# One block for TensorE's loop, a thirteenth turn, shorter programs, and octets loaded in pairs

## The chip, the cores and the metric

The kernel runs on one core of a Trainium2 chip. The metric is device time in microseconds for one execution; the time before is a median of three runs. The profile is of one further execution, and every duration below is from it unless another source is named.

## The reference

Linear attention with a ReLU feature map, on 8 batches x 12 heads, 512 positions, 64 dimensions, in float32:

```python
Q_feat = np.maximum(0, Q)
K_feat = np.maximum(0, K)
KV = np.einsum('bhkd,bhkv->bhdv', K_feat, V)
K_sum = np.sum(K_feat, axis=2)
numerator = np.einsum('bhqd,bhdv->bhqv', Q_feat, KV)
denominator = np.einsum('bhqd,bhd->bhq', Q_feat, K_sum)
return (numerator / (denominator[:, :, :, None] + 1e-10)).astype(np.float32)
```

## The kernel before, in words

The 96 heads are worked in twelve octets of eight heads (NO = 12). One octet of Q, K or V is 1 MiB in float32, laid out as 128 partitions of 32 rows each, so a partition holds 8 KB of the source and sixteen partitions hold one head. Q, K and V come in as bf16 (cast by the DMA), except K and V of octet 0, which come in as float32 on SyncE's and ScalarE's queues into output buffers that are not yet in use. All other loads go out on GpSimd's queue, one octet at a time (RUNS = (1,) * 11): three DMAs, K, V and Q, into a ring of six slots (RING); a load waits until the octet that used its slot has been consumed (semaphores PR1, VC, STG). Stores go out on GpSimd's queue too, except the last two, which SyncE issues. HEAD sets how many stores are put between the loads: in before, store 0 stands ahead of load 10 and store 1 ahead of load 11, and all others follow the last load. NOUT is the number of output buffers; norm(o) waits for store o - NOUT.

The program is written out by hand, engine by engine, with semaphores. There is no scheduler.

VectorE works in this order for each octet o: prep(o + 1, 0) masks the first half of K and part of V (after CK0, TensorE's sign that it is through with the buffers); stage(o + 1) copies Q to q_sb (STG); norm(o - 1) multiplies the transposed result by the reciprocals, in two halves (NRM0, NRM1), after TensorE's transposes (CB0, CB1); denominators(o) makes the reciprocals; prep(o + 1, 1) does the second halves (PR1). What stands behind a wait on VectorE waits too.

TensorE runs a hardware loop of twelve turns (lines 189 and 190). A turn transposes q_sb (16 matmuls, line 158), accumulates K'V in two halves of 32 (line 167), transposes back the result of the octet before (back, 16 matmuls, line 148, after OT), computes the denominators (line 176) and the numerators in two halves (line 184, after NRM0 and NRM1). After the loop stand two more back calls for the last octet. The loop's first instruction is placed at slot 0 of a block of 256 instructions (head_slot).

ScalarE evacuates the transposes of Q with the ReLU (line 214), K'V (line 219) and the numerators (ot, line 228), and masks a part of V (line 208).

At the end SyncE alone waits for the twelve store semaphores (line 318) and clears the semaphores; the other engines run off the end of their programs when their own work is done.

Of the kernel before, what the change touches and what calls it, by code (L numbers as in the profile page):

```python
# [5 lines left out]
def kernel(  # L6
# [5 lines left out]
):  # L12
    nc = tc.nc

    tc.close()
    tc.compile()

    B, H, S, D = Q.shape
    assert D == 64
    P = 128  # L20
    D1, D4 = D + 1, D + 4
    R = S * 4 // P
    RQ = 2 * R
    U = RQ // 2
    NO = B * H // 8
    assert NO * 8 == B * H and R == 16
    RING = 6
    NOUT = 9
    RUNS = (1,) * 11
    HEAD = 4  # L30

    fp32 = mybir.dt.float32
    bf16 = mybir.dt.bfloat16
    Act = mybir.ActivationFunctionType
    Alu = mybir.AluOpType
    PE, PL, VE, AC, SP = nc.tensor, nc.gpsimd, nc.vector, nc.scalar, nc.sync
# [6 lines left out]
    def sb(name, shape, dt):  # L43
        return nc.alloc_sbuf_tensor(name, shape, dt)[:]
# [3 lines left out]
    def sems(*names):  # L48
        new = [nc.alloc_semaphore(n) for n in names]
        handles.extend(new)  # L50
        return new

    ident = sb("ident", [P, P], bf16)
    ident32 = sb("ident32", [P, P], fp32)
    mask_k = sb("mask_k", [P, 2], fp32)
    mask_v = sb("mask_v", [P, 2], fp32)
    mask_h = sb("mask_h", [P, 8, 2], fp32)
    k_all = sb("k_all", [P, RING, RQ, D], bf16)
    v_all = sb("v_all", [P, RING, RQ, D], bf16)
    q_all = sb("q_all", [P, RING + 1, U * P], bf16)  # L60
    o_sb = [sb(f"o_sb{i}", [P, RQ, D], fp32) for i in range(NOUT)]
    k8, v8 = o_sb[0], o_sb[1]
# [1 line left out]
    q_sb = sb("q_sb", [P, U, P], bf16)  # L64
    qt_sb = sb("qt_sb", [P, U, P], bf16)
    kf = [sb(f"kf{i}", [P, R, 2, D], bf16) for i in range(2)]
    vo = [sb(f"vo{i}", [P, R, 2, D4], bf16) for i in range(2)]
    kvd = sb("kvd", [P, 8, 2 * D1], bf16)
    ot = sb("ot", [P, U, 8, 16], fp32)
    own = sb("own", [P, U, 8, 2], fp32)  # L70
# [10 lines left out]
    ID, STG, PR0, PR1, DEN, NRM0, NRM1, DV = sems(  # L81
        "id", "stg", "pr0", "pr1", "den", "nrm0", "nrm1", "dv")
    VC, KVD, OT = sems("vc", "kvd", "ot")
    CQ0, CQ1, CK0, CK1, CB0, CB1, CD, CO0, CO1 = sems(
        "cq0", "cq1", "ck0", "ck1", "cb0", "cb1", "cd", "co0", "co1")
    landed = {}
    stored = sems(*[f"st{o}" for o in range(NO)])

    def land(name):
        landed[name], = sems(name)  # L90
        return landed[name]


    SP.dma_start(out=k8.rearrange("p r d -> p (r d)"), in_=Kr[0]).then_inc(land("k0"), 16)
# [4 lines left out]
    def slot(o):  # L99
        return (o - 1) % RING if o > 0 else RING  # L100
# [13 lines left out]
    def store(eng, o):  # L114
        eng.wait_ge(NRM1, o + 2)
        kw = {"single_packet": True} if eng is PL else {}
        eng.dma_start(out=Or[o], in_=o_sb[(o + 2) % NOUT].rearrange("p r d -> p (r d)"), **kw).then_inc(stored[o], 16)  # L117

# [4 lines left out]
    o, done = 1, 0  # L123
    for n in RUNS:
        while done < o + n - 1 - RING - HEAD + 1:
            store(PL, done)
# [3 lines left out]
    assert o == NO  # L130
    for i in range(done, NO - 2):
        store(PL, i)
    for i in range(NO - 2, NO):
        store(SP, i)

# [2 lines left out]
    def arrived(eng, c, o):  # L138
        s = landed[f"{c}{run_of[o]}"]
        if (eng.engine, s.num) not in seen:  # L140
            seen.add((eng.engine, s.num))
            eng.wait_ge(s, 16)

    def back(j):
        for v in range(8):
            t = PE.transpose(ps_o[j][:, P * v:P * v + P], ot[:, 8 * j + v].rearrange("p h c -> p (h c)"), ident32)  # L148
        t.then_inc((CB0, CB1)[j], 1)
# [35 lines left out]
                              start=True, stop=True, skip_group_check=True)  # L185
            t.then_inc((CO0, CO1)[j], 1)

    PE.wait_ge(ID, 4)
    with nc.Fori(1, NO + 1, engines=bass.OrderedEngineSet([PE.engine]), head_slot={PE.engine: 0}) as i:
        turn(i)  # L190
    PE.wait_ge(OT, NO + 1)
    back(0)
    back(1)


    def v_rows(o, g):
        rows = slice(R * g, R * g + R)
        return v_all[:, slot(o), rows] if o > 0 else v8[:, rows]

    def k_rows(o, g):  # L200
        rows = slice(R * g, R * g + R)
        return k_all[:, slot(o), rows] if o > 0 else k8[:, rows]

    def v_scalar(o):
        arrived(AC, "v", o)
        if o == 0:
            AC.wait_ge(ID, 4)
        AC.activation(vo[0][:, :, 1, 2:D + 2], v_rows(o, 0), Act.Copy, scale=mask_v[:, 1:2]).then_inc(VC, 1)  # L208

    v_scalar(0)  # L210
    for o in range(NO):
        for j in range(2):
# [4 lines left out]
        for s in range(2):  # L217
            for c in range(2):
                t = AC.copy(  # L219
                    kvd[64 * c:64 * c + 64, s::2, c * D1:c * D1 + D1].rearrange("p (g t) d -> p g t d", t=2),  # L220
                    ps_kv[64 * s:64 * s + 64, :, 0:2 * (D + 2)].rearrange(
                        "p g (t d) -> p g t d", t=2)[:, :, :, c:c + D1])
# [3 lines left out]
        for j in range(2):  # L226
            AC.wait_ge((CO0, CO1)[j], o + 1)
            t = AC.copy(ot[:, :, 4 * j:4 * j + 4],  # L228
                        ps_o[j].rearrange("p (h u c) -> p u h c", h=4, u=U))
        t.then_inc(OT, 1)  # L230


    def prep(o, g):

        arrived(VE, "k", o)
        for s in range(2):
            VE.tensor_scalar(kf[g][:, :, s, :], k_rows(o, g), scalar1=0.0,  # L237
                             scalar2=mask_k[:, s:s + 1], op0=Alu.max, op1=Alu.mult)
        arrived(VE, "v", o)
        for t in range(1 + g):  # L240
            x = VE.tensor_scalar(vo[g][:, :, t, 2:D + 2], v_rows(o, g), scalar1=mask_v[:, t:t + 1],  # L241
                                 scalar2=None, op0=Alu.mult)
        x.then_inc((PR0, PR1)[g], 1)

    def stage(o):
        arrived(VE, "q", o)
        VE.tensor_copy(q_sb.rearrange("p u f -> p (u f)"), q_all[:, slot(o)]).then_inc(STG, 1)  # L247

    def norm(o):
        dst = o_sb[(o + 2) % NOUT]  # L250
        if o >= NOUT:
            VE.wait_ge(stored[o - NOUT], 16)
        VE.wait_ge(DV, 2 * o + 2 + DV0)
        if o == NOUT - 1:
            VE.wait_ge(VC, 1)
        for j in range(2):
            rs = slice(R * j, R * j + R)
            VE.wait_ge((CB0, CB1)[j], o + 2)
            VE.tensor_tensor(dst[:, rs], ps_o[j].rearrange("p (r d) -> p r d", d=D),  # L259
                             rec[o % 2][:, rs].unsqueeze(2).to_broadcast([P, R, D]),  # L260
                             op=Alu.mult).then_inc((NRM0, NRM1)[j], 1)

    def denominators(o):
        VE.wait_ge(CD, o + 1)
        VE.scalar_tensor_tensor(
            own.rearrange("p u h c -> p u (h c)"), ps_den.rearrange("p u h c -> p u (h c)"), 1e-10,
            mask_h.rearrange("p h c -> p (h c)").unsqueeze(1).to_broadcast([P, U, 16]),
            op0=Alu.add, op1=Alu.mult).then_inc(DEN, 1)
        VE.wait_ge(DEN, o + 2)
        VE.tensor_reduce(out=den.rearrange("p (u c) -> p u c", c=2), in_=own.rearrange("p u h c -> p u c h"),  # L270
                         op=Alu.add, axis=mybir.AxisListType.X).then_inc(DV, 1)
        VE.wait_ge(DV, 2 * o + 1 + DV0)
        VE.reciprocal(rec[o % 2], den).then_inc(DV, 1)

    for t in range(2):
        VE.memset(mask_v[:, t:t + 1], 0.0)
    VE.memset(kvd.rearrange("p h d -> p (h d)").bitcast(fp32), 0.0)
    VE.memset(ot.rearrange("p u h c -> p (u h c)"), 0.0).then_inc(OT, 1)
    ones = [vo[g][:, :, :, 1:D4 - 1][:, :, :, 0:D + 2:D1] for g in range(2)]
    VE.memset(ones[0], 0.0)  # L280
    VE.memset(ones[1], 0.0).then_inc(DV, 1)
    VE.wait_ge(DV, 1)
    for t in range(2):
        for half in range(2):
            b = 64 * half + 32 * t
            VE.memset(mask_v[b:b + 32, t:t + 1], 1.0)
            for g in range(2):
                VE.memset(ones[g][b:b + 32, :, t], 1.0)
    VE.wait_ge(ID, 2)
    VE.tensor_copy(ident32, ident).then_inc(ID, 1)  # L290
    VE.wait_ge(ID, 3)
    for c in range(2):
        VE.tensor_reduce(out=mask_h[:, :, c], in_=ident32.rearrange("p (h b) -> p h b", h=8),
                         op=Alu.add, axis=mybir.AxisListType.X)
    VE.tensor_reduce(out=mask_k, in_=ident32.rearrange("p (t s b) -> p s t b", t=4, s=2),
                     op=Alu.add, axis=mybir.AxisListType.XY).then_inc(ID, 1)
    DV0 = 1
    VE.wait_ge(ID, 4)
    for s in (DEN, NRM0, NRM1):
        VE.sem_inc(s, 1)  # L300
    prep(0, 0)
    prep(0, 1)
    stage(0)
    for o in range(NO):
        if o + 1 < NO:
            VE.wait_ge(CK0, o + 1)
            prep(o + 1, 0)
            stage(o + 1)
        if o > 0:
            norm(o - 1)  # L310
        denominators(o)
        if o + 1 < NO:
            prep(o + 1, 1)
    norm(NO - 1)


    for s in stored:
        SP.wait_ge(s, 16)
    used = sorted(s.num for s in handles)
    assert used == list(range(used[0], used[-1] + 1))  # L320
    SP.sem_clear(range(used[0], used[-1] + 1))
# [28 lines left out]
```

## Time and profile before

| What | Value |
|---|---|
| Median of three runs | 124.86 us (124.73 to 124.92) |
| Profiled execution, its time | 124.66 us |
| Its span (first to last instruction) | 123.4 us |
| Granted TensorE clock, mean | 0.941 |
| Busy: TensorE, VectorE, ScalarE, GpSimd | 71%, 72%, 64%, 22% |
| DMA | 32.57 MB moved in packets; HBM read 37.75 MB, written 12.58 MB |
| Loads on GpSimd's queue, issue to landing | 33 to 37 us (median by tensor) |
| SyncE's wait for the last stores (line 318) | 5.8 us |

The page gives for each engine the busy time and a row of 40 slices of the span; the DMA row is the mean busy share of the core's 16 DMA engines. A cast load is counted by the bytes that it writes, so that 213 GB/s in the middle of the row stand for twice as much read from HBM. Line numbers are those of the kernel before.

### The profile page before, as it was taken

Reading aid. Unit: us, or ns where it says so; the run is one execution under the profiler, and the core shown is the slowest. Engines: PE = TensorE matmul, PEld = TensorE weight load, DVE = VectorE, ACT = ScalarE, POOL = GpSimd, SP = SyncE. Lnnn points to the kernel's source line nnn. Section 1 sums busy time; section 2 is a strip of 40 time slices with the busy share of each in tenths; the row PEclk is TensorE's granted clock in tenths of the full one; section 3 lists DMA queues with packets and bytes.
Section 4 is the critical chain, followed back from the end, with each engine's and each line's share of the span. In section 5 each row is a group of like instructions: output and inputs, shape, how many; then the busy total and the mean of one; then the engine's idle time right before and its main releaser. Section 6 shows DMA issues by size and latency. Waiting matters only on the chain.

```text
span 123.4 us, 3380 instructions
## 1 busy us (share of the span) xinstructions
PE 87.4 (71%) x1456; PEld 75.9 (62%) x1456; DVE 89.3 (72%) x178; ACT 79.4 (64%) x109; POOL 27.5 (22%) x50
## 2 busy tenths in 40 slices
PE   0000099998998979799897998979449939977400
PEld 0000099986886868688686877958429928947200
DVE  3737906599989899998989989897395497091600
ACT  0043063999988888898888889888539649542000
POOL 3999500050240804309101001010010001000000
PEclk9999999999999999999999999999985995996775
DMA  3999999999999999999999999999999999999994
GB/s 43 369 344 217 213 213 213 213 215 213 214 213 213 213 215 213 214 214 217 214 213 214 213 214 221 371 217 214 375 222 214 343 425 428 425 422 433 420 425 170
DMA packets 6918, 32.57 MB, mean 264 GB/s; under 512 B 768, under 2 KB 768, under 8 KB 5120
## 3 DMA queue, kind: packets, MB, share of 16 engines
q0 software_dynamic: 6336, 28.31, 92.2%
q1 hardware_dynamic: 432, 3.15, 6.6%
q10 hardware_dynamic: 144, 1.05, 2.2%
q8 instruction: 2, 0.03, 0.1%
q14 instruction: 4, 0.03, 0.1%
HBM read 37.75 MB, written 12.58 MB: 408 GB/s over the span
## 4 chain that ended last, share of the span: by engine, by line
DMA 34%; issue 27%; POOL 18%; PE 8%; DVE 5%; ACT 1%; POOLq 0%; DVEq 0%
DMA q_all<-in_Q_dram 34%; POOL k_all L109 6%; POOL q_all L109 5%; POOL v_all L109 5%; DVE o_sb L259 5%; PE ps_o L148 4%; PE ps_kv L167 2%; PE ps_q L158 1%; PE ps_o L184 1%; POOL out_dram L117 1%; ACT ot L228 1%; POOL q_all L96 1%; POOL ident L121 0%; POOL ident L119 0%; POOLq L107 0%
## 5 line engine op out<-in xcount | busy, mean ns | idle before, releaser
L259 DVE TENSOR_TENSOR o_sb<-ps_o,rec 128x1024 f32<-128x1024 f32 x24 | 28.3, 1219 | 7.0 <-PE ps_o L148 6.7
L228 ACT COPY ot<-ps_o 128x1024 f32<-128x1024 f32 x24 | 24.2, 1013 | 10.3 <-PE ps_o L184 9.2
L167 PE MATMUL ps_kv<-vo,kf 64*128 64x132 bf16 x768 | 28.6, 230 | 0.7
L148 PE MATMUL ps_o<-ident,ot 128*128 128x128 f32 x208 | 27.1, 286 | 1.1 <-ACT ot L228 1.1
L167 PEld LDWEIGHTS ps_kv<-vo,kf 64*128 64x128 bf16 x768 | 24.8, 100 | 3.8 <-DVE vo L241 2.3
L214 ACT ACTIVATE qt_sb<-ps_q 128x1024 bf16<-128x1024 bf16 x24 | 23.4, 1030 | 5.1 <-PE ps_q L158 5.1
L158 PE MATMUL ps_q<-ident,q_sb 128*128 128x128 bf16 x192 | 15.3, 243 | 15.4 <-DVE q_sb L247 15.4
L148 PEld LDWEIGHTS ps_o<-ident,ot 128*128 128x128 f32 x208 | 23.8, 146 | 2.7 <-ACT ot L228 1.4
L158 PEld LDWEIGHTS ps_q<-ident,q_sb 128*128 128x128 bf16 x192 | 13.2, 110 | 16.7 <-DVE q_sb L247 15.4
L219 ACT CAST kvd<-ps_kv 64x260 bf16<-64x260 f32 x48 | 18.0, 375 | 7.8 <-PE ps_kv L167 7.4
L184 PE MATMUL ps_o<-qt_sb,kvd 128*128 128x256 bf16 x96 | 15.0, 282 | 10.8 <-DVE o_sb L259 9.8
L237 DVE TENSOR_SCALAR kf<-k_all,mask_k 128x1024 bf16<-128x1024 bf16 x44 | 18.3, 459 | 5.6 <-PE ps_kv L167 5.4
L184 PEld LDWEIGHTS ps_o<-qt_sb,kvd 128*128 128x128 bf16 x96 | 7.7, 100 | 15.6 <-DVE o_sb L259 15.0
L241 DVE TENSOR_SCALAR vo<-v_all,mask_v 128x1024 bf16<-128x1024 bf16 x33 | 15.0, 483 | 0.9 <-DMA v_all<-in_V_dram 0.9
L109 POOL DMA_DIRECT2D k_all<-in_K_dram x11 | 8.4, 763 | 32.1 <-DVE vo L241 32.0
L117 POOL DMA_DIRECT2D out_dram<-o_sb x10 | 5.3, 533 | 40.7 <-DVE o_sb L259 40.7
L208 ACT ACTIVATE vo<-v_all,mask_v 128x1024 bf16<-128x1024 bf16 x11 | 12.7, 1155 | 0.3
L247 DVE COPY q_sb<-q_all 128x2048 bf16<-128x2048 bf16 x12 | 8.3, 694 | 5.7 <-DMA q_all<-in_Q_dram 5.7
L109 POOL DMA_DIRECT2D q_all<-in_Q_dram x11 | 8.9, 811 | 0.0
L109 POOL DMA_DIRECT2D v_all<-in_V_dram x11 | 7.6, 687 | 0.0
L176 PE MATMUL ps_q<-kvd,qt_sb 128*128 128x16 bf16 x192 | 6.9, 180 | 0.0
L176 PEld LDWEIGHTS ps_q<-kvd,qt_sb 128*128 128x128 bf16 x192 | 6.7, 96 | 0.2
(24 smaller groups left out, 27.8 us busy)
## 6 DMA issues: line engine op xcount, KB each, us to landing
out_dram<-o_sb POOLq DMA_DIRECT2D x10, 1024.0 KB, 39.8
q_all<-in_Q_dram POOLq DMA_DIRECT2D x12, 512.0 KB, 36.7
k_all<-in_K_dram POOLq DMA_DIRECT2D x11, 512.0 KB, 33.1
v_all<-in_V_dram POOLq DMA_DIRECT2D x11, 512.0 KB, 34.8
out_dram<-o_sb SPq DMA_DIRECT2D x2, 1024.0 KB, 8.4
o_sb<-in_K_dram SPq DMA_DIRECT2D x1, 1024.0 KB, 8.5
o_sb<-in_V_dram ACTq DMA_DIRECT2D x1, 1024.0 KB, 8.8
```

Of the source, the lines that this page charges most:

```text
L109: PL.dma_start(out=t[:, to:to + n], in_=X[o:o + n].rearrange("n p f -> p n f"), single_packet=True).then_inc(land(f"{c}{o}"), 16)
L148: t = PE.transpose(ps_o[j][:, P * v:P * v + P], ot[:, 8 * j + v].rearrange("p h c -> p (h c)"), ident32)
L158: t = PE.transpose(dst[:, u], q_sb[:, j * (U // 2) + u], ident)
L167: t = PE.matmul(ps_kv[:, half, 0:2 * (D + 2)].rearrange("p (t d) -> p t d", t=2), kf[g][rows, r].rearrange("p s d -> p (s d)"), vo[g][rows ...
L176: t = PE.matmul(ps_den[:, u], qt_sb[:, u], kvd[:, :, 0:2 * D1:2 * D1 - 1], start=True, stop=True, skip_group_check=True)
L184: t = PE.matmul(ps[:, h], kvd[:, 4 * j + h, 1:2 * D + 1], q[:, :, 4 * j + h, :], start=True, stop=True, skip_group_check=True)
L214: AC.activation(qt_sb[:, j * (U // 2):(j + 1) * (U // 2)], ps_q[j].bitcast(bf16).rearrange("p (u f) -> p u f", u=U // 2), Act.Relu)
L219: t = AC.copy(kvd[64 * c:64 * c + 64, s::2, c * D1:c * D1 + D1].rearrange("p (g t) d -> p g t d", t=2), ps_kv[64 * s:64 * s + 64, :, 0:2 * ...
L228: t = AC.copy(ot[:, :, 4 * j:4 * j + 4], ps_o[j].rearrange("p (h u c) -> p u h c", h=4, u=U))
L237: VE.tensor_scalar(kf[g][:, :, s, :], k_rows(o, g), scalar1=0.0, scalar2=mask_k[:, s:s + 1], op0=Alu.max, op1=Alu.mult)
L241: x = VE.tensor_scalar(vo[g][:, :, t, 2:D + 2], v_rows(o, g), scalar1=mask_v[:, t:t + 1], scalar2=None, op0=Alu.mult)
L259: VE.tensor_tensor(dst[:, rs], ps_o[j].rearrange("p (r d) -> p r d", d=D), rec[o % 2][:, rs].unsqueeze(2).to_broadcast([P, R, D]), op=Alu. ...
```

## The change

The program of each engine is altered, not what is computed.

- TensorE: an alignment to a block of 256 instructions is put ahead of the opening barrier, so that barrier, loop and end stand in one block; the alignment at the loop head and the wait on ID ahead of it go. The loop has thirteen turns, and the last octet's back calls are those of turn 13. So that turn 13 can pass its waits, VectorE raises STG, PR0 and PR1 once more after the last denominators, and ScalarE raises KVD and VC after its last copy.
- VectorE: the masks of V and the ones beside V are made with one reduction and one copy instead of sixteen memsets; three semaphore increments ride on instructions that are there anyway; norm waits for DV only for the last octet, and prep waits for DV at its second V mask instead. The program goes from 211 to 186 instructions.
- GpSimd: octets 3 and 4, 5 and 6, 7 and 8 are loaded two by two, one DMA each for K, V and Q of a pair (RUNS); one store (HEAD 5) instead of two stands ahead of the last loads. The program goes from 68 to 59 instructions.
- NOUT goes from 9 to 11. Stores 1 to 9 share the semaphore ALL, stores 10 and 11 share LAST.
- End: TensorE, ScalarE, VectorE and GpSimd wait for all stores too (hold) and raise FIN; SyncE waits for FIN.

```diff
+    nc.tensor.addr_align(256, offset=0, max_nops=0)
     tc.close()
     tc.compile()
...
-    NOUT = 9
-    RUNS = (1,) * 11
-    HEAD = 4
+    NOUT = 11
+    RUNS = (1, 1, 2, 2, 2, 1, 1, 1)
+    HEAD = 5
...
-    vo = [sb(f"vo{i}", [P, R, 2, D4], bf16) for i in range(2)]
+    vo_all = sb("vo", [P, 2, R, 2, D4], bf16)
+    vo = [vo_all[:, i] for i in range(2)]
...
-    stored = sems(*[f"st{o}" for o in range(NO)])
+    ALL, LAST, FIN = sems("all", "last", "fin")
+    stored = [sems(f"st{o}")[0] if o + NOUT < NO else ALL if o < NO - 2 else LAST for o in range(NO)]
...
+    def hold(eng):
+        eng.wait_ge(ALL, 16 * (NOUT - 2))
+        eng.wait_ge(LAST, 32)
+        eng.sem_inc(FIN, 1)
...
+    hold(PL)
...
-    PE.wait_ge(ID, 4)
-    with nc.Fori(1, NO + 1, engines=bass.OrderedEngineSet([PE.engine]), head_slot={PE.engine: 0}) as i:
+    with PE.Fori(1, NO + 2) as i:
         turn(i)
-    PE.wait_ge(OT, NO + 1)
-    back(0)
-    back(1)
+    hold(PE)
...
+    AC.wait_ge(KVD, NO)
+    AC.wait_ge(VC, NO)
+    AC.sem_inc(KVD, 1)
+    AC.sem_inc(VC, 1)
+    hold(AC)
...
         for t in range(1 + g):
+            if t and o:
+                VE.wait_ge(DV, 2 * o + DV0)
...
-        VE.wait_ge(DV, 2 * o + 2 + DV0)
+        if o == NO - 1:
+            VE.wait_ge(DV, 2 * o + 2 + DV0)
...
-    for t in range(2):
-        VE.memset(mask_v[:, t:t + 1], 0.0)
...
+    VE.tensor_reduce(out=mask_v, in_=ident32.rearrange("p (a t b) -> p t a b", a=2, t=2),
+                     op=Alu.add, axis=mybir.AxisListType.XY).then_inc(ID, 1)
...
+    VE.tensor_copy(vo_all.rearrange("p g r t d -> p (g r) t d")[:, :, :, 1:D4 - 1][:, :, :, 0:D + 2:D1],
+                   mask_v.unsqueeze(1).unsqueeze(3).to_broadcast([P, 2 * R, 2, 2])).then_inc(ID, 1)
...
+    for s in (STG, PR0, PR1):
+        VE.wait_ge(s, NO)
+        VE.sem_inc(s, 1)
     norm(NO - 1)
-    for s in stored:
-        SP.wait_ge(s, 16)
+    hold(VE)
+    SP.wait_ge(CO1, NO + 1)
+    SP.wait_ge(FIN, 4)
```

More of the change, by code (lines that the diff above doesn't have):

```diff
@@ L206, in v_scalar @@
         if o == 0:
-            AC.wait_ge(ID, 4)
+            AC.wait_ge(ID, 5)
         AC.activation(vo[0][:, :, 1, 2:D + 2], v_rows(o, 0), Act.Copy, scale=mask_v[:, 1:2]).then_inc(VC, 1)
@@ L273, in denominators @@
         VE.reciprocal(rec[o % 2], den).then_inc(DV, 1)
-    for t in range(2):
-        VE.memset(mask_v[:, t:t + 1], 0.0)
-    VE.memset(kvd.rearrange("p h d -> p (h d)").bitcast(fp32), 0.0)
+    VE.memset(kvd.rearrange("p h d -> p (h d)").bitcast(fp32), 0.0).then_inc(DEN, 1)
     VE.memset(ot.rearrange("p u h c -> p (u h c)"), 0.0).then_inc(OT, 1)
[L279 to L288, printed above, removed]
     VE.wait_ge(ID, 2)
@@ L291 @@
     VE.wait_ge(ID, 3)
-    for c in range(2):
-        VE.tensor_reduce(out=mask_h[:, :, c], in_=ident32.rearrange("p (h b) -> p h b", h=8),
-                         op=Alu.add, axis=mybir.AxisListType.X)
+    VE.tensor_reduce(out=mask_v, in_=ident32.rearrange("p (a t b) -> p t a b", a=2, t=2),
+                     op=Alu.add, axis=mybir.AxisListType.XY).then_inc(ID, 1)
     VE.tensor_reduce(out=mask_k, in_=ident32.rearrange("p (t s b) -> p s t b", t=4, s=2),
-                     op=Alu.add, axis=mybir.AxisListType.XY).then_inc(ID, 1)
-    DV0 = 1
+                     op=Alu.add, axis=mybir.AxisListType.XY).then_inc(NRM0, 1)
+    VE.tensor_reduce(out=mask_h, in_=ident32.rearrange("p (h b) -> p h b", h=8).unsqueeze(2).to_broadcast([P, 8, 2, 16]),
+                     op=Alu.add, axis=mybir.AxisListType.X).then_inc(NRM1, 1)
     VE.wait_ge(ID, 4)
-    for s in (DEN, NRM0, NRM1):
-        VE.sem_inc(s, 1)
+    VE.tensor_copy(vo_all.rearrange("p g r t d -> p (g r) t d")[:, :, :, 1:D4 - 1][:, :, :, 0:D + 2:D1],
+                   mask_v.unsqueeze(1).unsqueeze(3).to_broadcast([P, 2 * R, 2, 2])).then_inc(ID, 1)
+    DV0 = 0
+    VE.wait_ge(ID, 5)
     prep(0, 0)
```

## The prediction

> **What bounds it now.** I read the page's span and DMA rows, the windows of the last microseconds, the DMA packet and semaphore records of the trace, the timeline of a steady octet and the chain that ended last.
>
> ```profile
> span 123.4 us, 3380 instructions
> ...
> DMA  3999999999999999999999999999999999999994
> ...
> q8 instruction: 2, 0.03, 0.1%
> q14 instruction: 4, 0.03, 0.1%
> ```
>
> DMA is full from the second slice to the last: the kernel runs at DMA pace, and only the ends can give anything. The end is not sharp. In the windows (columns: stretch, length, busy per engine, PEclk, DMA share, GB/s):
>
> ```profile
> 120.00:121.00 1.00, 0.00 (x0) 0.00 (x0) 0.00 (x0) 0.00 (x0) 0.00 (x0) 0.50 0.99 418
> 121.00:121.50 0.50, 0.00 (x0) 0.00 (x0) 0.00 (x0) 0.00 (x0) 0.00 (x0) 0.50 0.59 246
> 121.50:122.00 0.50, 0.00 (x0) 0.00 (x0) 0.00 (x0) 0.00 (x0) 0.00 (x0) 0.50 0.20 82
> 122.00:122.50 0.50, 0.00 (x0) 0.00 (x0) 0.00 (x0) 0.00 (x0) 0.00 (x0) 0.50 0.20 82
> ```
>
> A fifth to a quarter of the 16 engines work 1.2 us longer than the rest. The packet records say why: instruction fetches. TensorE's queue q8 moved 16384 B at 11.50 (0.94 us) and at 114.34 (0.97 us); q14 moved 8192 B at 32.7, 49.7, 97.5, 105.5 (0.31 to 0.32 us each). The semaphore records follow the damage: octet 0's Q lands on all 16 engines within 0.3 us, from the next load on one engine is 1.2 us late on every load, and the last store lands on twelve engines by 121.92 and on four at 122.67, 122.69, 123.04, 123.13. The program ends 0.23 us after that.
>
> The compute loop has no room either. One octet of VectorE, and the tail of the chain:
>
> ```profile
> 49.94 2.36 DVE L259 TENSOR_TENSOR o_sb<-ps_o,rec 128x1024 f32<-128x1024 f32 x2
> ...
> 56.56 0.69 DVE L247 COPY q_sb<-q_all 128x2048 bf16<-128x2048 bf16 x1 [0.30 <-DMA q_all<-in_Q_dram]
> 57.28 1.22 DVE L259 TENSOR_TENSOR o_sb<-ps_o,rec 128x1024 f32<-128x1024 f32 x1
> ```
>
> ```profile
> 106.60 1.04 PE ps_o L148 x8
> 107.64 0.03 issue
> 107.67 0.05 DVEq L258
> 107.72 0.04 issue
> 107.76 2.37 DVE o_sb L259 x2
> ...
> 111.89 3.50 PE ps_o L148 x16
> 115.39 0.02 issue
> 115.41 1.23 DVE o_sb L259
> ```
>
> From one norm to the next is 7.33 us (49.94 to 57.28; 35.29 to 79.28 is six such). Norm 2.28, denominators 1.17, prep(o+1, 1) 1.58, TensorE's second half 1.1 and transposes 1.2 make it, whatever DMA does. Three MiB at 2.457 us each (the step between landings) are 7.37 us. So time lost by the compute side early is hardly won back.
>
> **The change, part by part.** Sums are made in the profiled execution: 124.66 us, 1.30 more than its span; it lies 0.2 below the median of 124.86, and the forecast is the median less the gain.
>
> *TensorE's block.* Before puts the loop's head at slot 0 of a block of 256 instructions; the loop has 244, so the 16 transposes behind it (32) cross into the next block. They ran from 111.89 on at an even 213 ns step (half clock) with no gap, while the fetch at 114.34 came later: so a fetch brings the block after the one entered. The change enters one block at the start, keeps loop and thirteenth turn in it, and its `hold` stays there. Both 16 KB fetches leave the busy stretch; one moves to the start, about 1 us ahead of or beside the first packets (2.4 us, which take 1.1 us anyway). Cost there: 0 to 1.2 us on one engine; I take 0.3, as those packets wait for latency, not for rate.
> The row first: even transposes across a block edge say that the block stood ready. [...]
>
> *Shorter programs.* VectorE 211 to 186 instructions, GpSimd 68 to 59. The fetches at 97.5 and 105.5 fit the end of VectorE's program and GpSimd's last store (101.8); with `hold` they should go. Two 8 KB ones stay, 0.31 us on one engine each.
>
> *Pairs.* GpSimd's 34 loads become 25. The step of a MiB is 2.457 us, its eight packets 8 x 0.305; the rest, 0.017 us, is paid nine times less: 0.15 us. DMA's own end: 121.2 (best engines) - 0.15 + 0.31 = 121.4, with 0.1 for one more block at the start 121.5, against 122.7.
>
> *What pairs cost.* Octet 3's Q lands with octet 4's: at 40.7 instead of 34.4. norm(1) stands behind stage(3) in VectorE's order, so it starts at 40.7 + 0.1 + 0.69 = 41.5 instead of 35.29; behind it wait the denominators, prep(3, 1) and TensorE (its idle stretch, 36.7 to 42.8, halves its clock as at 91.7). The like case is norm(8) at 89.28 after a wait: its next transposes began at 96.67, + 1.2 is 97.9, a loop of 8.6. From there data is early (Q of 5 and 6 at 55.5 with stage(5) due at 56.5; Q of 7 and 8 at 70.4, due at 71) and loops go at compute pace. norm now waits once less: the separate wait at L258 (0.05 and its issue) goes, so 7.27. norm(10): 41.5 + 8.6 + 8 x 7.27 = 108.3, against 107.76. The loads of octets 10 and 11 come one store earlier (HEAD 5) and without the late engine, about 3.5 us, so they don't bind; NOUT 11 leaves only norm(11) waiting for a store that lands near 87.
>
> *Thirteenth turn.* Before the last transposes TensorE now does 16 of q_sb and 64 matmuls on stale data. STG is raised as the last reciprocal issues (norm(10) + 3.2); 1.06 (the 16 in steady state) + 2.1 (the 64) + two transposes groups, and norm's second half ends at + 9.9; before it was + 8.9, with transposes at half clock (3.50 against 1.97). So 118.2 against 116.64. What decides is the clock:
>
> ```profile
> 98.48:101.89 3.41, 1.53 (x26) 1.09 (x23) 3.33 (x5) 1.85 (x2) 0.12 (x1) 1.00 1.03 432
> 108.72:112.13 3.41, 1.66 (x18) 0.95 (x15) 2.50 (x5) 2.02 (x2) 0.00 (x0) 1.00 1.01 425
> ```
>
> Both stretches (TensorE busy 45 and 49%) were followed by half clock; steady ones of 82% were not. The turn's worst stretch holds about 74%: I take full clock; half would cost 1.4.
> [...]
>
> *Last store.* Issued at 118.25; its first packet comes 1.0 (octet 0's K, 1.40 to 2.41) to 1.7 us later (the last store of before, 116.67 to 118.38): 119.6; 2.46 of transfer: 122.05; 0.41 to the semaphore: 122.45. DMA would be free for it at 121.5 - 2.46 = 119.0, so compute, not DMA, ends by about half a microsecond.
>
> *End.* All engines wake, raise FIN, then SyncE: 0.23 becomes about 0.35 (two hops of about 0.06, the step between SyncE's waits). Bounds 0.05 and 0.4, as the engines now finish together. Span 122.8, time 124.1, gain 0.56: **124.3 us**. Set-up instructions of VectorE cost nothing: it waited 2.75 us for K before line 237. The added wait on DV in prep is long met. GpSimd's later loads (7 and 8 wait for prep(2, 1), near 33) are due only at 55.
>
> **Rivals.**
> 1. *Compute starves DMA, slower.* The pair's 6.2 us plus cold loop are not won back, and the turn falls to half clock or the loop stays at 7.33 (+0.5). Last store issued 1 to 1.9 us later than summed, DMA idle before it: 125.2 (124.6 to 126.2). It decides once norm(11) ends after about 118.9. For it: no slack in the loop. Against: HEAD and the freed wait.
> [...]
> 3. *No change.* The moved fetch makes one engine 1.2 us late from the start, as now: all loads of octets 3 and 4 and the end are late again, 124.8.
>
> **Chances.** Forecast 0.55, rival 1 0.23, rival 2 0.07, rival 3 0.15. Low end: DMA's own end binds, 121.5 + 0.41 + 0.35 + 1.3 = 123.55, 123.75 by the median; the block at the start and the hops at their low bounds make it 123.6. High end takes in most of rival 1: 125.5. A change of 0.2% (0.25 us) is about what can be told from none. Faster 0.55, same 0.15, slower 0.30.
>
> **What would show it.** Right: no 16384 B instruction packet after about 4 us, last store's landings within 0.5 us; q_sb copy of octet 3 near 41, norm(1) behind it, PEclk 0.5 there; then norms every 7.27; norm(11) ends near 118; DMA below full for half a microsecond near 119. Wrong: K's issue later than 1.5 us (rival 2); a late engine already at octet 1 (rival 3); norm(11) after 119 with half clock in the thirteenth turn (rival 1).

## The result, and the profile after

The changed kernel takes 126.73 us in the median of six runs (126.21 to 127.04); the kernel before took 124.76 us in six runs beside it (124.67 to 124.92). The ratio is 1.0146, with a 95% interval of 1.0128 to 1.0164. The forecast was 124.3 us, so the sign was wrong and the size by 2.4 us.

The profiled execution took 127.04 us. From the page of the kernel after:

```profile
span 124.1 us, 3556 instructions
...
DMA  1899999999999999999999999999999999999966
...
q8 instruction: 1, 0.02, 0.1%
q14 instruction: 2, 0.02, 0.0%
```

Two things are to be seen. The span grew from 123.4 to 124.1 us, while the time of this execution grew by 2.4 us: most of that lies outside the span (the time less the span), which was 1.3 us and is 2.9 us here. Four of the six runs have 2.3 and two have 2.9 (median 2.33), so by the medians about half of the loss lies there. And the DMA row, which was full up to its last slice, ends in two slices that are not.

The fetches did change as summed. The page lists one 16384 B packet and two of 8192 B within the span. The packet records put the first at 1.88 us and the two at 37.4 and 58.6; the old ones at 97.5, 105.5 and 114.3 are gone. A second packet of 16384 B follows at 126.33, behind the end of the span.

The timeline of VectorE, copies of Q and norms (start, length, instruction, idle time before it):

```profile
41.96 0.69 DVE L265 COPY q_sb<-q_all 128x2048 bf16<-128x2048 bf16 x1 [4.38 <-DMA q_all<-in_Q_dram]
42.56 2.35 DVE L278 TENSOR_TENSOR o_sb<-ps_o,rec 128x1024 f32<-128x1024 f32 x2
...
51.57 2.36 DVE L278 TENSOR_TENSOR o_sb<-ps_o,rec 128x1024 f32<-128x1024 f32 x2
...
58.84 2.36 DVE L278 TENSOR_TENSOR o_sb<-ps_o,rec 128x1024 f32<-128x1024 f32 x2 [0.35 <-PE ps_o L161]
...
109.74 2.36 DVE L278 TENSOR_TENSOR o_sb<-ps_o,rec 128x1024 f32<-128x1024 f32 x2 [2.31 <-PE ps_o L161]
```

VectorE waits 4.38 us for the pair's Q, and norm(1) starts at 42.56. The next loop takes 9.01 us, and then one norm follows the other every 7.27 us, waiting 0.35 us for TensorE and never for data. From 42 us on the compute chain sets its own pace, while DMA stays full until 118. The end of the chain that ended last:

```profile
109.74 2.36 DVE o_sb L278 x2
113.00 1.07 PE ps_q L171 x16
114.07 2.00 PE ps_kv L180 x64
116.07 1.04 PE ps_o L161 x8
117.24 2.37 DVE o_sb L278 x2
119.65 0.61 PE ps_o L197 x4
```

Before the last transposes (L161, from 116.07) stand the 16 transposes of q_sb and the 64 matmuls of the thirteenth turn. norm(11) ends at 119.60, the last store is issued at 119.62, and its first packet comes at 120.46. The windows (stretch, length, busy time of TensorE, of its weight loads, of VectorE, ScalarE and GpSimd, PEclk, DMA share, GB/s) show what DMA does meanwhile:

```profile
118.00:119.00 1.00, 0.86 (x19) 0.59 (x15) 1.00 (x2) 0.00 (x0) 0.00 (x0) 1.00 0.90 377
119.00:120.00 1.00, 0.48 (x6) 0.31 (x4) 0.59 (x1) 0.00 (x0) 0.00 (x0) 1.00 0.26 107
120.00:121.00 1.00, 0.26 (x3) 0.00 (x0) 0.00 (x0) 0.00 (x0) 0.00 (x0) 1.00 0.64 270
...
122.00:123.00 1.00, 0.00 (x0) 0.00 (x0) 0.00 (x0) 0.00 (x0) 0.00 (x0) 0.50 0.86 360
123.00:124.00 1.00, 0.00 (x0) 0.00 (x0) 0.00 (x0) 0.00 (x0) 0.00 (x0) 0.50 0.02 8
```

From 119 to 120 DMA is a quarter busy: it waits for the last store. Then all 16 DMA engines work together to 123, and the store lands on fifteen engines at 123.24 to 123.44 and on one at 123.83. So the end is sharp, as intended, but it is no earlier than the ragged end of before (123.13).

### The profile page after: what moved, and what is told of

Its sections match the earlier page's. It is cut to its first block, busy times and chain, and to the rows that moved or that the text cites. A ratio compares the mean times of both kernels' runs of the same rounds, so it can differ in the third digit from the quotient of the medians.

```text
span 124.1 us, 3556 instructions
## 1 busy us (share of the span) xinstructions
PE 90.4 (73%) x1560; PEld 78.0 (63%) x1560; DVE 87.6 (71%) x163; ACT 79.4 (64%) x109; POOL 22.4 (18%) x41
## 4 chain that ended last, share of the span: by engine, by line
DVE 38%; DMA 27%; PE 23%; POOL 5%; issue 2%; POOLq 0%; DVEq 0%
DMA q_all<-in_Q_dram 27%; DVE o_sb L278 21%; PE ps_kv L180 11%; PE ps_o L161 8%; DVE vo L259 5%; DVE kf L253 4%; DVE den L289 3%; DVE own L284 2%; DVE rec L292 2%; PE ps_q L171 2%; POOL k_all L120 1%; POOL v_all L120 1%; PE ps_o L197 1%; POOL q_all L120 1%; DVE q_sb L265 1%
## 5 line engine op out<-in xcount | busy, mean ns | idle before, releaser
L180 PE MATMUL ps_kv<-vo,kf 64*128 64x132 bf16 x832 | 31.0, 230 | 0.8
L180 PEld LDWEIGHTS ps_kv<-vo,kf 64*128 64x128 bf16 x832 | 26.8, 100 | 4.1 <-DVE vo L259 2.6
L161 PE MATMUL ps_o<-ident,ot 128*128 128x128 f32 x208 | 25.6, 276 | 0.0
L197 PE MATMUL ps_o<-qt_sb,kvd 128*128 128x256 bf16 x104 | 16.6, 286 | 12.1 <-DVE o_sb L278 11.4
L161 PEld LDWEIGHTS ps_o<-ident,ot 128*128 128x128 f32 x208 | 22.5, 141 | 1.5 <-issue 0.2
L197 PEld LDWEIGHTS ps_o<-qt_sb,kvd 128*128 128x128 bf16 x104 | 8.4, 101 | 17.6 <-DVE o_sb L278 15.6
L120 POOL DMA_DIRECT2D k_all<-in_K_dram x8 | 5.4, 678 | 46.4 <-DVE vo L259 46.2
L189 PE MATMUL ps_q<-kvd,qt_sb 128*128 128x16 bf16 x208 | 7.5, 180 | 0.0
L253 DVE TENSOR_SCALAR kf<-o_sb,mask_k 128x1024 bf16<-128x1024 f32 x4 | 2.8, 746 | 5.5 <-DMA o_sb<-in_K_dram 5.5
L284 DVE SCALAR_TENSOR_TENSOR own<-ps_q,mask_h 128x256 f32<-128x256 f32 x12 | 5.0, 416 | 2.2 <-PE ps_q L189 2.2
```

Of the source, the lines that this page charges most:

```text
L180: t = PE.matmul(ps_kv[:, half, 0:2 * (D + 2)].rearrange("p (t d) -> p t d", t=2), kf[g][rows, r].rearrange("p s d -> p (s d)"), vo[g][rows ...
L189: t = PE.matmul(ps_den[:, u], qt_sb[:, u], kvd[:, :, 0:2 * D1:2 * D1 - 1], start=True, stop=True, skip_group_check=True)
L197: t = PE.matmul(ps[:, h], kvd[:, 4 * j + h, 1:2 * D + 1], q[:, :, 4 * j + h, :], start=True, stop=True, skip_group_check=True)
```

## The experiments

The theory after the first result was that three costs make the loss: the start, the octets in pairs together with the thirteenth turn (compute ends after DMA has run dry), and hold (time outside the span). The rival was that one of them alone carries it. Each kernel below undoes one or more parts of the change, or does one part alone on the kernel before. The ratio is to the kernel before, run on the same chip; span and time outside the span are medians of 4 to 12 runs (the kernel before: 7 to 25), the latter the time less the span. Traces are of one execution each. Where a landing on "the middle engine" is given, it is the median of the transfer's 16.

| Kernel | Time, us | Ratio (95%) | Span | Outside |
|---|---|---|---|---|
| before | 124.84 to 124.94 | 1 | 123.6 | 1.33 |
| after | 126.73 | 1.0146 (1.0128 to 1.0164) | 124.15 | 2.33 |
| nohold | 126.14 | 1.0097 (1.0064 to 1.0130) | 124.45 | 1.70 |
| singles | 125.70 | 1.0054 (1.0034 to 1.0074) | 123.9 | 1.81 |
| nohold_singles | 125.49 | 1.0038 (1.0006 to 1.0070) | 124.1 | 1.40 |
| loophead | 126.25 | 1.0101 (1.0083 to 1.0120) | 123.95 | 2.30 |
| loophead_singles_nohold | 125.00 | 1.0001 (0.9985 to 1.0017) | 123.55 | 1.44 |
| after12 | 126.26 | 1.0092 (1.0067 to 1.0118) | 124.3 | 1.96 |
| before_hold | 125.19 | 1.0016 (0.9993 to 1.0039) | 123.6 | 1.66 |
| before_pairs | 125.04 | 0.9995 (0.9975 to 1.0016) | 123.7 | 1.30 |
| before_pairs_hold | 125.58 | 1.0054 (1.0034 to 1.0074) | 123.6 | 2.01 |
| before_13 | 124.78 | 0.9983 (0.9963 to 1.0002) | 123.5 | 1.30 |
| before_early | 124.87 | 0.9991 (0.9978 to 1.0004) | 123.55 | 1.32 |
| pe_free | 126.90 | 1.0163 (1.0135 to 1.0191) | 124.45 | 2.35 |
| pl_only | 126.13 | 1.0118 (1.0087 to 1.0149) | 124.1 | 2.03 |
| pe_only | 126.33 | 1.0124 (1.0091 to 1.0157) | 124.55 | 1.78 |
| ve_only | 126.24 | 1.0113 (1.0066 to 1.0160) | 124.55 | 1.68 |
| ac_only | 126.00 | 1.0087 (1.0053 to 1.0120) | 124.35 | 1.68 |

### hold, pairs, and both taken out

**nohold**: the four hold calls go, SyncE waits for the stores itself.

```diff
-    hold(PL)   # and hold(PE), hold(AC), hold(VE)
-    SP.wait_ge(FIN, 4)
+    SP.wait_ge(ALL, 16 * (NOUT - 2))
+    SP.wait_ge(LAST, 32)
```

> The changed kernel (126.73) without hold: SyncE alone waits for ALL and LAST. Theory A (three terms: 0.4 us at the start from TensorE's taken branch, about 0.3 us net of DMA idle before the last store because pairs delay the compute, and 1.0 to 1.6 us outside the span because four engines begin their epilogue only when the stores are in): time less span falls from 2.3-2.9 to about 1.3 us, time 125.3 to 125.7, span 124.0 or up to 0.9 more if a fetch of TensorE's next block lands on one DMA engine under the last store. Theory B (the time outside the span is TensorE's fetch of a 16384 B block, seen at 126.33, wherever TensorE stands): the fetch moves to about 121 and the time outside falls, but the span grows by up to 1 us: 126.2 to 126.6. Theory C (pairs are nearly all of the loss, hold costs nothing): unchanged, 126.5 to 126.8.

**singles**: octets are loaded one by one again.

```diff
-    RUNS = (1, 1, 2, 2, 2, 1, 1, 1)
+    RUNS = (1,) * 11
```

> The changed kernel with octets loaded one by one again (RUNS = (1,) * 11), all else kept. Theory A: norm(1) starts near 35.7 instead of 42.6, the last norm ends before 118, the last store follows at DMA pace: span about 123.3, time outside the span still 2.3 to 2.9, time 125.6 to 126.1. Theory C: time 124.7 to 125.0. If the program of GpSimd crosses a block again, one 8192 B fetch comes back late, 0.3 us on one DMA engine.

**nohold_singles**: both edits.

> Both: singles and no hold. Theory A: only the start's 0.4 us and one DMA engine about 0.9 us late are left of the change's costs, and two 8192 B fetches less: span 123.2 to 123.8, 1.3 outside, 124.5 to 125.1, the same as before within 0.3. Theory C: as singles alone, 124.7 to 125.0 with about 2.5 outside the span.

**before_hold**: hold put into the kernel before (each engine waits for the twelve store semaphores), SyncE waits for FIN.

> The kernel before with one thing added: TensorE, ScalarE, VectorE and GpSimd wait for all twelve stores at their end and raise FIN, SyncE waits for FIN. Theory A: span 123.4 plus 0.1, time outside the span from 1.3 to 2.3-2.9, time 125.8 to 126.5. Theory B: TensorE has crossed its block already, its fetch stays at 114 under the stores, so time outside stays 1.3: 124.8 to 125.0. Theory C: 124.8 to 125.0.

Without hold the time is 126.14, 0.6 less than in the changed kernel, and all of that lies outside the span (1.70 for 2.33). With single loads it is 125.70, 1.0 less, half of it outside the span too (1.81); with both 125.49. On the kernel before, hold costs 0.16% with an interval that holds zero, though the time outside its span goes from a median of 1.33 to 1.66, and its ten runs (1.51 to 1.79) all lie above the kernel before (1.26 to 1.44). So hold is a part of the loss and not the whole, and what it costs depends on the kernel that it is put into.

Theory A came closest but missed in three of the four: nohold and nohold_singles are slower than it said (by 0.4 us over its upper bound), and before_hold is faster by 0.6 than its lower bound. Singles came out in its range, but with 1.81 outside the span for 2.3 to 2.9. The fetch that theory B puts at 121 is not in the trace of nohold.

### The start

**loophead**: the alignment ahead of the barrier goes, and the loop of thirteen turns is placed at slot 0 of a block, as in the kernel before.

```diff
-    nc.tensor.addr_align(256, offset=0, max_nops=0)
...
-    with PE.Fori(1, NO + 2) as i:
+    with nc.Fori(1, NO + 2, engines=bass.OrderedEngineSet([PE.engine]), head_slot={PE.engine: 0}) as i:
```

> The changed kernel without the aligned block at the start; the loop of thirteen turns stands at the head of a block of its own, as the loop of before does. Theory: the start's 0.42 us is the branch that TensorE takes ahead of the opening barrier, so K's issue is back at 1.40, the drain at 0.83; the 16384 B fetch comes at 2.3 to 2.6, when TensorE enters the loop at once, and one engine is 0.9 to 1.2 us late as now. norm(11) at 116.8 (117.24 less 0.42), time 126.2 to 126.4. Rival: the start's 0.42 us lies beside transfers that set norm(1) anyway, and the time stays at 126.6 to 126.8.

The first load in the timeline, in the kernel after:

```profile
1.82 0.38 SPq L105 DMA_DIRECT2D o_sb<-in_K_dram  x1
```

and in loophead:

```profile
1.39 0.38 SPq L104 DMA_DIRECT2D o_sb<-in_K_dram  x1
```

0.43 us comes back at the start, and the time falls by 0.48, though the median span by 0.2 only. A second pair is cleaner: nohold_singles and loophead_singles_nohold differ in the block at the start alone, and there time falls by 0.49 and span by 0.55. The instruction records show where it was: a COMPARE_BRANCH of TensorE at 0.826 that lasts 309 ns, its next instruction at 1.194, all ahead of the barrier that every engine waits for. In loophead the same branch stands at 1.57, behind the barrier, and nobody waits for it. The branch does not wait for the fetch, whose packet starts at 1.88, when TensorE has long gone on.

One expectation failed. The fetch did not come at 2.3 to 2.6 but at 5.19, and norm(1) was no earlier (42.86).

### Pairs alone and the thirteenth turn alone

**before_pairs**: RUNS alone, on the kernel before.

> The kernel before with the loads of octets 3 to 8 two by two (RUNS alone). Theory: the pairs are the largest part of the loss: norm(1) goes from 35.3 to about 41.7 to 42, the loops after it take 7.33 us, and the kernel ends on the compute chain: norm(11)'s second half at 115.4 or later, last store issued 0.5 to 2 us later than 116.67, DMA below full in the last 4 us; time 125.6 to 126.4, 0.7 to 1.5 more than before. Rival: the loops of before wait for data that come late on one engine, so pairs only move idle time and the time stays within 0.3 of before (124.7 to 125.2).

The theory said 0.7 to 1.5 us more; the time is the same (0.9995). The norms are late, as expected (norm(1) even a little more: 42.52 for 41.7 to 42):

```profile
42.52 2.35 DVE L259 TENSOR_TENSOR o_sb<-ps_o,rec 128x1024 f32<-128x1024 f32 x2
...
109.85 2.36 DVE L259 TENSOR_TENSOR o_sb<-ps_o,rec 128x1024 f32<-128x1024 f32 x2 [2.34 <-PE ps_o L148]
115.20 2.36 DVE L259 TENSOR_TENSOR o_sb<-ps_o,rec 128x1024 f32<-128x1024 f32 x2 [1.83 <-PE ps_o L148]
```

but the windows at the end show that it does not matter yet:

```profile
118.00:119.00 1.00, 0.00 (x0) 0.00 (x0) 0.00 (x0) 0.00 (x0) 0.00 (x0) 1.00 1.05 442
119.00:120.00 1.00, 0.00 (x0) 0.00 (x0) 0.00 (x0) 0.00 (x0) 0.00 (x0) 1.00 1.03 434
120.00:121.00 1.00, 0.00 (x0) 0.00 (x0) 0.00 (x0) 0.00 (x0) 0.00 (x0) 0.50 0.95 401
121.00:122.00 1.00, 0.00 (x0) 0.00 (x0) 0.00 (x0) 0.00 (x0) 0.00 (x0) 0.50 0.45 188
```

norm(11) ends at 117.56, 0.9 later than in the kernel before, and its store still joins a full DMA. The last store lands at 121.73 on the middle engine and at 123.48 on the latest. The late engines end the kernel, and compute had room up to them.

**before_13**: the thirteenth turn alone, on the kernel before.

```diff
-    with nc.Fori(1, NO + 1, engines=bass.OrderedEngineSet([PE.engine]), head_slot={PE.engine: 0}) as i:
+    with nc.Fori(1, NO + 2, engines=bass.OrderedEngineSet([PE.engine]), head_slot={PE.engine: 0}) as i:
         turn(i)
-    PE.wait_ge(OT, NO + 1)
-    back(0)
-    back(1)
...
+    AC.sem_inc(KVD, 1)   # and VC on ScalarE; STG, PR0 and PR1 on VectorE; SyncE also waits for CO1
```

> The kernel before with the thirteenth turn alone (ScalarE and VectorE raise what it waits for; the loop stands at slot 0 of its block as before; no pairs, no hold). Theory: without pairs there is room for it: norm(11) ends at 117.5 to 118.7 in place of 116.64, the last store is still issued before DMA runs dry, the fetch at 114.3 is gone and one or two fewer engines are late: span 122.8 to 123.3, time 124.2 to 124.7. Rival: the turn is on the path here too; the last store is issued 1.5 to 2 us later and the time is 125.2 or more.

0.9983, with an interval that just holds 1: neither the gain nor the loss. The last store is issued at 118.76, 2.1 later than before. The windows show a smaller gap than in the changed kernel:

```profile
119.00:120.00 1.00, 0.40 (x4) 0.11 (x2) 0.00 (x0) 0.00 (x0) 0.00 (x0) 1.00 0.69 287
120.00:121.00 1.00, 0.00 (x0) 0.00 (x0) 0.00 (x0) 0.00 (x0) 0.00 (x0) 0.79 1.01 426
121.00:122.00 1.00, 0.00 (x0) 0.00 (x0) 0.00 (x0) 0.00 (x0) 0.00 (x0) 0.50 0.93 393
```

In the gap the late engines catch up in part: the store lands at 122.48 in the middle and 123.24 at the latest. The middle engine is 0.7 later than with pairs alone, the latest 0.2 earlier. One limit has taken the other's place.

**after12**: the changed kernel with twelve turns and the back calls behind the loop, as before.

> The changed kernel with twelve turns and the two transpose groups behind the loop, as before; pairs, hold, the block at the start and the shorter programs stay. Theory: the thirteenth turn takes 2.0 us of the chain (norm(11) ends at 119.60 in the changed kernel and at 117.56 with pairs alone, where DMA is full to 121). Here norm(11) ends at about 117.6 to 117.9, the last store is issued 1.8 to 2.0 us earlier, DMA has no gap near 119, and the landings are at 121.8 to 122.0 on most engines; the transposes behind the loop bring a 16384 B fetch near 116 and one to three engines land at 122.6 to 123.3. Time 125.2 to 125.8, and less than 2.3 us outside the span. Rival: the loss lies in hold and the start; the time stays at 126.3 to 126.8.

The time falls by 0.5 only, and the expected 117.6 to 117.9 for norm(11) was missed: it ends at 119.76. Its norm(10) starts at 110.82, 1.1 later than in the changed kernel: in this execution the late engine brings the pair's Q at 43.52 (41.93 there). TensorE's transposes run at half clock (PEclk 0.50 from 116 to 118, full with pairs alone), and the store is issued at 119.78, no earlier than with thirteen turns. So this run does not price the turn by itself, and the gap near 119 is there without it (DMA share 0.28 from 119 to 120). It shows that the fetch behind the loop is back (16384 B at 117.1) and that the time outside the span is 1.96 for 2.33.

### Where the late engine comes from

**before_early**: the kernel before without TensorE's wait ahead of its loop.

```diff
-    PE.wait_ge(ID, 4)
     with nc.Fori(1, NO + 1, engines=bass.OrderedEngineSet([PE.engine]), head_slot={PE.engine: 0}) as i:
```

> The kernel before without TensorE's wait for the identity ahead of its loop, so that it enters the loop's block at once; nothing else is changed. Theory: the first 16384 B fetch moves from 11.5 to 2.3 to 2.6 us and costs one engine 0.9 to 1.2 us as it did, so the four late engines at the end stay and the time stays within 0.3 of before (124.7 to 125.2). Rival, from the prediction: beside the first packets the fetch is paid by waiting for latency, the engine is on time (0.3 us late), fewer engines are late at the last landing, and the time falls to 124.3.

The fetch moved from 11.5 to 5.29, not to 2.3, and the time did not move (0.9991). The last store lands at 123.46 on the latest engine, and at 123.13 in the kernel before. A fetch at 5.29 spares nothing. It doesn't test the rival's condition, a fetch beside the first packets, since those start at 2.41.

**loophead_singles_nohold**: the changed kernel without the block at the start, without pairs and without hold. What stays are the thirteenth turn, the shorter programs and the eleven buffers.

> The changed kernel without the block at the start, without pairs and without hold: what stays are the thirteenth turn, the shorter programs, eleven output buffers and the loop entered at once. Theory: start, pairs and hold are the whole loss, so the time is at or below that of before, 124.5 to 125.0, with the last store landing by 122.0 on most engines and one engine 0.9 to 1.2 us late from the first loads on; 1.4 us outside the span. Rival: the thirteenth turn costs by itself; 125.3 or more.

The time is that of the kernel before, 1.0001. Start, pairs and hold are thus the whole loss, and what is left gains nothing that can be measured. It has no gap (the chain ends early: norm(11) starts at 113.14, the last store is issued at 115.52) and no fetch at 114, and the windows of its end look like those of the kernel before:

```profile
120.00:121.00 1.00, 0.00 (x0) 0.00 (x0) 0.00 (x0) 0.00 (x0) 0.00 (x0) 0.62 1.10 467
121.00:122.00 1.00, 0.00 (x0) 0.00 (x0) 0.00 (x0) 0.00 (x0) 0.00 (x0) 0.50 0.38 156
122.00:123.00 1.00, 0.00 (x0) 0.00 (x0) 0.00 (x0) 0.00 (x0) 0.00 (x0) 0.50 0.10 41
```

Two engines in place of four are late, but the latest lands at 123.43. The semaphore records show one engine 1.7 us late on every load from 13 to 35 us, where it is 0.9 to 1.0 in the changed kernel, 1.9 in nohold_singles and 1.2 in the kernel before. In each of them the lag begins with the first load that lands after the first 16384 B fetch. Packet records don't name the engine; that the late engine is the one that carried the fetch is inferred from this order.

How late it is goes with how far the fetch reaches into the first load. Ten kernels have the block at the start, and their first load's packets start at 2.83 to 2.92. In nohold the fetch is over at 2.79, and the engine is 0.6 us late on the loads behind it; in the changed kernel it is over at 2.88 (0.96 us late in the median), in pe_free at 3.08 (1.6), in nohold_singles at 3.19 (1.9), in after12 at 3.39 (2.5). The five others lie between, nearly in this order.

### Outside the span

**before_pairs_hold**: pairs and hold, on the kernel before.

> The kernel before with both pairs and hold, nothing else. The time outside the span was 1.3 us with pairs alone, 1.65 with hold alone, 2.3 in the changed kernel. Theory: hold costs outside the span by how late all engines are let go at once, so about 1.65 here, time 125.2 to 125.5. Rival: hold costs more where GpSimd's program is shorter (25 loads for 34), whatever ends the span: then 2.3 here too, time 125.8 to 126.2.

**pe_free**: the changed kernel without hold(PE) alone.

> The changed kernel with hold left out on TensorE alone (SyncE then counts three). The runs so far put the time outside the span at 1.3 us before, 1.65 with hold on the kernel before, 1.7 in the changed kernel without any hold and 2.3 to 2.9 in the changed kernel. Theory: what is above 1.7 is TensorE, which in the changed kernel goes past its block only when hold lets it go, so that a 16384 B fetch (at 126.33) falls behind the end. Then this kernel has no such fetch, 1.7 to 2.0 us outside the span and a time of 126.0 to 126.3. Rival: it is the joint end of all engines; then the fetch is gone and the time stays at 126.5 to 126.8, with 2.3 or more outside the span.

**pl_only, pe_only, ve_only, ac_only**: the changed kernel with the hold of one engine alone, SyncE waiting for one FIN.

> The changed kernel with hold on GpSimd alone. Theory: GpSimd's hold makes the time outside the span, since hold cost 0.33 us with single loads and 0.7 with pairs, and pairs shorten GpSimd's program and no other: 2.2 to 2.4 us outside the span here, time 126.5 to 126.9, while the other three runs of this set stay at 1.7. Rival: every held engine has the same way to go after its release; then each of the four runs has 2.0 to 2.4.

> The changed kernel with hold on TensorE alone. Theory (GpSimd's hold): 1.7 us outside the span, time 126.0 to 126.3. Rival (any held engine): 2.0 to 2.4, time 126.4 to 126.8; a 16384 B fetch behind the end again.

> The changed kernel with hold on VectorE alone. Theory (GpSimd's hold): 1.7 us outside the span, time 126.0 to 126.3. Rival (any held engine): 2.0 to 2.4, time 126.4 to 126.8.

> The changed kernel with hold on ScalarE alone. Theory (GpSimd's hold): 1.7 us outside the span, time 126.0 to 126.3. Rival (any held engine): 2.0 to 2.4, time 126.4 to 126.8.

Both answers to before_pairs_hold were wrong: 2.01 us lies between 1.65 and 2.3 (its seven runs reach from 1.67 to 2.08). Pairs alone add nothing outside the span (1.30), hold alone 0.33, both 0.7. TensorE's late fetch is not the cause: without hold(PE) nothing is gained (2.35). GpSimd's hold alone brings 1.70 to 2.03, half of what all four bring, and less than the 2.2 to 2.4 of its theory; the other three alone bring 0.08, -0.02 and -0.02, as its theory said. The other half needs more than one held engine.

The page ends with the span, but the trace's semaphore records go on behind it. There some 240 semaphores change one after another within 0.6 to 0.8 us. The first of them changes 0.24 to 0.30 us after the end of the span in the ten kernels whose GpSimd is not held, and 0.44 to 0.59 in the eight where it is; pl_only has 0.56, nohold 0.26. This 0.30 is nearly all of what GpSimd's hold alone brings. What makes the other half stays open, and so does why the changed kernel without hold has 1.70, where pairs alone and the thirteenth turn alone have 1.30.

## Why the prediction was wrong

The forecast is missed by 2.4 us, and two steps of the sum make it. The last store was to be issued at 118.25 and to land at 122.45; it was issued at 119.62 and landed at 123.83, 1.4 later, which is the compute chain alone, since issue to landing was summed right (4.2). And the time outside the span was to stay at 1.30; it is 2.33, 1.03 more.

**Time outside the span (wrong).** The sum took 1.30 us for what lies around the span, as in the kernel before, and put hold at 0.12 inside the span (0.23 to 0.35). Inside it was right: the landing at 123.83 is followed by the end at 124.07, 0.24 later. But the time outside grew by 1.03 us, and the sum took it as fixed. The step that failed is "Span 122.8, time 124.1": 1.30 was added without a reason why it should stay. About 0.6 of the 1.03 is hold (nohold has 1.70), and 0.3 goes with pairs (nohold_singles has 1.40); by which mechanism stays open. The runs show no one figure for it: the kernels' medians reach from 1.30 (before_pairs, before_13) to 2.35 us (pe_free).

**Start (mis-sized).** Forecast 0.1 us for DMA and none for the compute chain; measured 0.42 at K's issue, 0.48 in the time. It is the branch ahead of the barrier (309 ns, and 0.37 us from its start to TensorE's next instruction). K's issue at 1.82 is past the 1.5 that the prediction gave as the sign of rival 2, but no fetch is waited for: the packet starts at 1.88, behind K's issue.

**Moved fetch (mis-sized, and it carried the gain).** Forecast 0.3 us late on one engine, measured 0.9 to 1.0 on the loads from 13 to 35 us, though the packet (1.88 to 2.88) is over just after the first load begins (2.83). This is rival 3's mechanism. Nearest to 0.3 comes nohold (0.6), whose fetch is over before the first load's packets; where a run's fetch reaches further into them its engine is later, up to 2.5 us (after12). The first packets are slow indeed (0.77 to 1.18 us for the 8192 B of each of the first sixteen in the kernel before, 0.31 to 0.33 for those of the same load from 3.86 us on), but the reason made of it, that they wait for latency and not for rate, did not make a fetch that reaches into them cheap. The bounds of 0 to 1.2 held the measured lag; the 0.3 taken was the mis-sized term. "DMA's own end 121.5" therefore holds for most engines (121.9 in loophead_singles_nohold) and not for the latest (123.4). The gain of 1.2 us from a common end had only one of its two conditions. The 0.15 us that pairs were to save DMA is not seen either: with pairs alone the last store lands on the middle engine at 121.73, in the kernel before at 121.76.

**The later fetches (right in number, not in cause).** The fetches at 97.5 and 105.5 went, as summed, but not through hold: nohold has neither, and before_hold has both (97.6 and 105.6).

**The compute chain (right in its links, 1.4 us late by mis-sized terms).** Copy of octet 3: forecast 40.8, measured 41.96. The pair's Q lands on fifteen engines at 40.56 to 41.36 and on the late one at 41.93; the start's 0.42 and the late engine, both missing from this step, make up the delay. Cold loop: 8.6 against 9.01; the half clock lasted from 42.59 to 49.42, where the like case of before had 3.4 us. Loops: 7.27, measured 7.27. Thirteenth turn: +9.9 from norm(10) to the end of norm(11), measured 9.86, at full clock. norm(11) ends at 119.60 instead of 118.2, past the 118.9 from which rival 1 decides. The gap in the DMA windows is that rival, and its 1 to 1.9 us of delay was right, though neither half clock in the turn nor loops of 7.33 brought it. Pairs alone and the thirteenth turn alone leave the time where it was, while with the turn and the block at the start pairs cost 0.65 us (nohold 126.14, nohold_singles 125.49); whether the changed kernel would be free of the gap with twelve turns is not shown, since after12 has it too. Loads were in time, as summed.

**The clock (right).** The windows of the kernel after, with TensorE's busy time ahead of the others:

```profile
39.18:42.59 3.41, 0.00 (x0) 0.00 (x0) 0.63 (x2) 0.00 (x0) 0.00 (x0) 1.00 1.06 213
42.59:46.00 3.41, 2.07 (x10) 1.22 (x11) 3.34 (x6) 1.01 (x1) 0.00 (x0) 0.50 1.07 215
46.00:49.42 3.42, 3.42 (x51) 3.22 (x50) 1.58 (x5) 2.85 (x3) 1.54 (x3) 0.50 1.07 217
110.85:114.26 3.41, 2.55 (x37) 1.78 (x36) 2.35 (x5) 2.02 (x2) 0.00 (x0) 1.00 1.01 425
114.26:117.68 3.42, 3.42 (x77) 3.31 (x72) 0.44 (x1) 0.00 (x0) 0.00 (x0) 1.00 1.00 422
```

and of after12, without the thirteenth turn:

```profile
111.40:114.81 3.41, 1.82 (x26) 1.10 (x24) 2.88 (x5) 1.94 (x2) 0.00 (x0) 1.00 1.01 425
114.81:118.22 3.41, 3.27 (x16) 3.27 (x16) 1.17 (x1) 0.08 (x1) 0.00 (x0) 0.50 1.01 423
```

In the kernel after, half clock (PEclk 0.50) begins behind a window in which TensorE does nothing, and the thirteenth turn's window, 75% busy (2.55 of 3.41; forecast 74%), is followed by full clock (1.00). Without the turn the like window is 53% busy (1.82), and half clock (0.50) follows. So half clock came behind a window of 0% and behind one of 53%, and not behind the one of 75%.

**What the loss is made of.** Of the 1.97 us lost (126.73 less 124.76), the start is 0.48 (loophead). Outside the span lies 0.86 (2.30 in loophead, 1.44 in loophead_singles_nohold, where neither pairs nor hold are left), and 0.4 lies in the span (123.95 and 123.55). The DMA gap is the likely reason of the latter: loophead has it (DMA share 0.12 from 119 to 120), loophead_singles_nohold has not. This makes 1.74; the other 0.2 is within what the spans scatter. In the two runs of the changed kernel with 2.9 outside, the fetch at 126.33 (to 127.29) may be the reason: the profiled one is of these. There is one trace of each kernel, so this is not shown. No kernel here beats the kernel before by more than can be measured; before_13, at 0.9983, comes nearest.

## What to carry to other kernels

A kernel that two limits share, here a late DMA engine and a compute chain with about 2 us of room (before_13 issues its last store 2.1 us later and loses no time), cannot be improved by lifting one limit and spending the room of the other. Add up the room that all parts of a change spend before summing their gains: pairs alone and the turn alone were free, and in the changed kernel, which has both, pairs were not. And the time outside the span is not a constant: making engines wait for the last store cost 0.3 to 0.7 us that no row of the span shows.

## What the runs showed of the hardware

Behind an instruction fetch of 16384 B, whose packet takes 0.92 to 1.33 us, one of the 16 landings of every load from 13 to 35 us is 0.6 to 2.5 us later than their median (1.2 in the kernel before, 0.96 in the changed one). It is least late where the fetch is over before the first load's packets (nohold, 2.79 and 2.83), and most late where the fetch reaches 0.55 us into them (after12). In before_early, without a gap, the lag is 1.65 us on the loads and still 1.53 at the last store; in loophead, with a gap ahead of the last store, it goes from 1.6 to 0.59. Where TensorE enters its loop behind the opening barrier (in loophead its branch stands at 1.57 us), the fetch's packet starts at 5.19 (loophead) and 5.29 us (before_early), among the loads; in the ten kernels with the block at the start it starts at 1.86 to 2.47.

With GpSimd alone held until the last store has landed, the time outside the span is 0.33 us longer than without hold (pl_only 2.03, nohold 1.70); with TensorE, VectorE or ScalarE alone held it is 0.08 us longer or less (pe_only 1.78, ve_only and ac_only 1.68).
